# Output projection by seven block products for two token tiles, in place of eight

## The chip, the cores and the metric

The kernel runs on one core of one Trainium2 chip. The metric is the device time of one execution in microseconds (us); three runs of the kernel before took 950.98, 951.33 and 952.13 us, so the time before is the median, 951.33 us.

## What is computed

One decoder layer over 2048 tokens of width 1024, in fp32. A linear recurrence (HGRN2, four heads of 128) gives the first 512 columns of `mix`, sliding-window attention gives the other 512. Then comes the part that the change is about:

```python
mix = jnp.concatenate([o_h, o_a], axis=-1)            # (T, 1024)
out = jnp.einsum('bte,ed->btd', mix, w_out[layer])     # 1024 x 1024
z = DN_ALPHA * h_res.astype(f32) + out.astype(f32)
mu = jnp.mean(z, axis=-1, keepdims=True)
var = jnp.mean(jnp.square(z - mu), axis=-1, keepdims=True)
z = (z - mu) * lax.rsqrt(var + LN_EPS)
h_res = (z * ln_g[layer].astype(f32) + ln_b[layer].astype(f32)).astype(dt)
```

`o_h` is multiplied by a weight per column before; the kernel puts that weight (`hgw_s`) into the first four row blocks of `w_out`.

## The kernel before

The kernel works in three stages: attention (two key/value heads, four token blocks of 512 each), the recurrence (two pairs of heads, index `j`, again four token blocks `b`), and the output stage (16 token tiles of 128). The first two leave their results in DRAM tiles (`sw_spill`, `hg_spill`); the output stage reads them back.

All projections split both fp32 operands into a high part in the fp32r format and a low part, the remainder. A product is three matmuls: high by high, high by low, low by high. ScalarE makes the high part by a copy into fp32r (L97), VectorE or GpSimd subtracts for the low part (L98).

In the output stage `prepare(n)` (L333) loads one token tile `m` with four DMAs from SyncE's queue (L336, L337), has TensorE transpose the four recurrence blocks into PSUM (L342), and splits the eight blocks into `mh` and `ml` (L343 to L346). A token tile then has two halves of 512 output columns; each is a chain of 24 matmuls of 128x128 by 128x512 into one PSUM bank (L537 to L539, eight row blocks `e` by three). VectorE adds the residual (L540, `xr` is loaded by L513), takes statistics (L541, L543), GpSimd makes the reciprocal root (L545, L546), VectorE normalizes with two operations per half (L550, L551), and ScalarE's queue stores (L553, L555). The last token tile is cut into 512, 256 and 256 columns.

The eight row blocks of `w_out` are loaded and split by `load_wo` (L349): six of them, and the first `prepare`, are written into the last step of the recurrence (L421, L422, at `j == 1`, the last block, `pr == 1`), the other two behind it (L509). They go into the buffers of the recurrence's weights (pool `wp`, eight buffers) and tokens (pool `xp`, seven). Every raw tile, of weights, of tokens and of `m`, passes through `rawp`, 4 KB per partition and three buffers.

The order of work on each engine is not the order of the source. A planner simulates a time line when the kernel is built (`schedule_with_timeline_sim=True`): among the instructions that are ready it takes the one that stands first in the source. Buffers of one tag are given out in the order of the source, so the tile n of a tag waits until tile n - bufs is released. Each engine then runs its list in that order.

The projection of the recurrence's values in the last block (`vg`, L120 to L122) reads the weights `wv` in four buffers of `wp`, and `xs` in four of `xp`. After it come, per pair of token tiles, the masked products `ap` (L444, L447), the transposes `kp` (L454), the state update `hkv` (L475), and the outputs `ho` (L488, L492).

Of the kernel before, what the change touches and what calls it, by code (L numbers as in the profile page):

```python
# [10 lines left out]
F32 = mybir.dt.float32  # L11
# [6 lines left out]
P = 128  # L18
# [21 lines left out]
def tile_hybrid_layer(  # L40
# [17 lines left out]
    rawp = ctx.enter_context(tc.tile_pool(name="rawp", bufs=3))  # L58
    wp = ctx.enter_context(tc.tile_pool(name="wp", bufs=8))
# [122 lines left out]
    hk = ctx.enter_context(tc.tile_pool(name="shared", bufs=2))  # L182
# [150 lines left out]
    def prepare(n):  # L333
        m = rawp.tile([P, 8, P], F32, tag="raw", name=f"m{n}")
        for j in range(2):
            nc.sync.dma_start(m[:, 2 * j : 2 * j + 2, :], hg_spill[n // 2][j][n % 2])  # L336
            nc.sync.dma_start(m[:, 4 + 2 * j : 6 + 2 * j, :], sw_spill[n][j])  # L337
        mh = xp.tile([P, 8, P], F32R, tag="xh", name=f"mh{n}")
        ml = xp.tile([P, 8, P], F32R, tag="xl", name=f"ml{n}")
        mp = tr_ps(f"mp{n}")  # L340
        for e in range(4):
            nc.tensor.transpose(mp[:, e, :], m[:, e, :], ident)  # L342
        nc.scalar.activation(mh[:, 0:4, :], mp, AF.Copy)  # L343
        nc.vector.tensor_sub(ml[:, 0:4, :], mp, mh[:, 0:4, :].bitcast(F32))
        nc.scalar.activation(mh[:, 4:8, :], m[:, 4:8, :], AF.Copy)
        nc.vector.tensor_sub(ml[:, 4:8, :], m[:, 4:8, :], mh[:, 4:8, :].bitcast(F32))  # L346
        return mh, ml

    def load_wo(e):  # L349
        pool, tag = (wp, "w") if e < 4 else (xp, "x")  # L350
        return load_split(wo[e], pool, tag, f"wo{e}", scale=hgw_s[:, e : e + 1] if e < 4 else None)

# [1 line left out]
    with (  # L354
# [9 lines left out]
        for j in range(2):  # L364
# [4 lines left out]
            for b in range(NTB):  # L369
# [49 lines left out]
                for pr in range(NBLK // 2):  # L419
                    if j == 1 and b == NTB - 1 and pr == 1:  # L420
                        ws = [load_wo(e) for e in range(6)]  # L421
                        ahead = prepare(0)  # L422
# [86 lines left out]
    ws += [load_wo(e) for e in range(6, 8)]  # L509
    with tc.tile_pool(name="outp", bufs=2, reuse_waits="tile") as wk:  # L510
        def load_res(n):
            xr = wk.tile([P, D], F32, tag="xr", name=f"xr{n}")
            nc.sync.dma_start(xr, xn[n * P : (n + 1) * P, :])  # L513
            return xr

        xrs = [load_res(0), load_res(1)]
        lg = wk.tile([P, D], F32, name="lg", bufs=1)
        nc.sync.dma_start(lg, lng.to_broadcast([P, D]))
        lbt = wk.tile([P, D], F32, name="lbt", bufs=1)
        nc.sync.dma_start(lbt, lnb.to_broadcast([P, D]))  # L520
        for n in range(T // P):
            mh, ml = ahead
            if n + 1 < T // P:
                ahead = prepare(n + 1)
            last = n + 1 == T // P
            xr = xrs.pop(0)
            if n + 2 < T // P:
                xrs.append(load_res(n + 2))
            z = wk.tile([P, D], F32, tag="z", name=f"z{n}")
            cuts = [0, 512, 768, 1024] if last else [0, 512, 1024]  # L530
            stats = wk.tile([P, len(cuts) - 1, 6], F32, tag="bst", name=f"bst{n}")
            for i, (c0, c1_) in enumerate(zip(cuts, cuts[1:])):
                c = slice(c0, c1_)
                ps = mm_ps(f"po{n}_{i}")[:, : c1_ - c0]
                for e in range(8):
                    wh, wl = ws[e]
                    nc.tensor.matmul(ps, lhsT=mh[:, e, :], rhs=wh[:, c], start=e == 0, stop=False)  # L537
                    nc.tensor.matmul(ps, lhsT=mh[:, e, :], rhs=wl[:, c], start=False, stop=False)  # L538
                    nc.tensor.matmul(ps, lhsT=ml[:, e, :], rhs=wh[:, c], start=False, stop=e == 7)  # L539
                nc.vector.scalar_tensor_tensor(z[:, c], xr[:, c], ALPHA, ps, op0=ALU.mult, op1=ALU.add)  # L540
                nc.vector.bn_stats(stats[:, i, :], z[:, c])  # L541
            mv = wk.tile([P, 2], F32, tag="mv", name=f"mv{n}")
            nc.vector.bn_aggr(mv, stats)  # L543
            rs = wk.tile([P, 1], F32, tag="rs", name=f"rs{n}")
            nc.gpsimd.tensor_scalar(rs, mv[:, 1:2], LN_EPS, None, op0=ALU.add)  # L545
            nc.gpsimd.tensor_tensor(rs, rs, mhalf[:, 0:1], op=ALU.pow)  # L546
            y = wk.tile([P, D], F32, tag="y", name=f"y{n}")
            for half in range(2):
                c = slice(half * 512, (half + 1) * 512)
                nc.vector.scalar_tensor_tensor(y[:, c], z[:, c], mv[:, 0:1], lg[:, c], op0=ALU.subtract, op1=ALU.mult)  # L550
                nc.vector.scalar_tensor_tensor(y[:, c], y[:, c], rs, lbt[:, c], op0=ALU.mult, op1=ALU.add)  # L551
                if last:
                    nc.scalar.dma_start(out[n * P : (n + 1) * P, c], y[:, c])  # L553
# [72 lines left out]
```

## Time and profile before

| what | value |
|---|---|
| median of three runs | 951.33 us |
| the profiled execution | span 951.3 us; the runs show no time outside it that could be told apart (median less span: 0.03 us) |
| TensorE busy | 933.0 us, 98% |
| VectorE busy | 607.3 us, 64% |
| ScalarE busy | 308.4 us, 32% |
| GpSimd busy | 322.0 us, 34% |
| the chain that ended last | TensorE 85%, VectorE 6%, DMA 4%, ScalarE 3% |
| matmuls L537, L538, L539 | 264 each (248 with 512 columns and 16 with 256) |

In rows of the profile, PE is TensorE's matmul, PEld its weight load, DVE VectorE, ACT ScalarE, POOL GpSimd, SP SyncE; a q behind a name is that engine's queue. L12 is line 12 of the kernel. Matmuls overlap in the pipeline, so the time from start to start counts, not the length of one.

### The profile page before, as it was taken

What the parts mean: (1) busy time and instruction counts of PE and PEld (TensorE: products, weight loads), DVE (VectorE), ACT (ScalarE), POOL (GpSimd) and SP (SyncE); (2) the same over time, 40 slices, a digit from 0 to 9 for tenths busy, and PEclk for the clock granted to TensorE, in tenths of its full rate; (3) what the DMA queues carried; (4) which work ended last, traced back from release to release, by engine and by line L of the source; (5) the groups of instructions that cost most, each with busy time, mean ns of one, the idle gap of its engine ahead of it and who ended that gap; (6) DMA issues with size and microseconds to landing.
All of it is one profiled execution on the core that took longest, in us unless ns stands there. A gap on an engine that the chain in (4) does not pass through costs nothing.

```text
span 951.3 us, 12917 instructions
## 1 busy us (share of the span) xinstructions
PE 933.0 (98%) x4744; PEld 750.7 (79%) x4744; DVE 607.3 (64%) x1233; ACT 308.4 (32%) x785; POOL 322.0 (34%) x306
## 2 busy tenths in 40 slices
PE   8999999999998999999999999999999989999996
PEld 7878777777786777878887887888788878888885
DVE  5877887867879955726366383726458446666554
ACT  5455545544564423131142423122133211000000
POOL 1645536445447534313042642313133111111111
PEclk9999999999999999999999999999999999999998
DMA  7423243033242403002032321103013253444321
GB/s 261 165 72 123 70 158 124 33 106 106 78 151 94 127 12 101 23 12 100 1 122 78 100 100 65 47 1 102 10 56 123 78 188 134 143 152 146 113 99 57
DMA packets 33216, 91.03 MB, mean 96 GB/s; under 512 B 4224, under 2 KB 12416, under 8 KB 33152
## 3 DMA queue, kind: packets, MB, share of 16 engines
q1 hardware_dynamic: 27792, 73.41, 23.7%
q0 software_dynamic: 2912, 8.40, 2.5%
q10 hardware_dynamic: 2448, 8.39, 2.2%
q8 instruction: 37, 0.61, 0.3%
q14 instruction: 27, 0.22, 0.1%
HBM read 73.41 MB, written 16.78 MB: 95 GB/s over the span
## 4 chain that ended last, share of the span: by engine, by line
PE 85%; DVE 6%; DMA 4%; ACT 3%; issue 1%; SPq 0%; POOL 0%; POOLq 0%; DVEq 0%; ACTq 0%
PE vg L121 6%; PE vg L120 6%; PE vg L122 6%; PE po L537 6%; PE po L539 6%; PE po L538 6%; PE fp L110 3%; PE fp L111 3%; PE fp L112 3%; PE hq L112 3%; PE hq L110 3%; PE hq L111 3%; PE op L320 3%; PE qp L112 2%; PE qp L110 2%; PE qp L111 2%
## 5 line engine op out<-in xcount | busy, mean ns | idle before, releaser
L537 PE MATMUL po<-wo_h,mh 128*128 128x512 f32 (+1 forms) x264 | 103.1, 391 | 2.8 <-DVE z L540 2.8
L539 PE MATMUL po<-wo_h,ml 128*128 128x512 f32 (+1 forms) x264 | 102.0, 386 | 0.0
L538 PE MATMUL po<-wo_l,mh 128*128 128x512 f32 (+1 forms) x264 | 101.9, 386 | 0.0
L120 PE MATMUL vg<-wh_h,xh_h 128*128 128x512 f32 x256 | 100.8, 394 | 0.0
L121 PE MATMUL vg<-wh_l,xh_h 128*128 128x512 f32 x256 | 100.8, 394 | 0.0
L122 PE MATMUL vg<-wh_h,xh_l 128*128 128x512 f32 x256 | 100.7, 394 | 0.0
L98 POOL TENSOR_TENSOR xh_l<-xh_raw,xh_h 128x1024 fp32r<-128x1024 f32 x16 | 39.1, 2448 | 125.6 <-ACT xh_h L97 122.9
L540 DVE SCALAR_TENSOR_TENSOR z<-xr,po 128x512 f32<-128x512 f32 (+1 forms) x33 | 22.1, 672 | 70.3 <-PE po L539 64.3
L545 POOL TENSOR_SCALAR rs<-mv 128x1 f32<-128x1 f32 x16 | 9.4, 584 | 151.4 <-DVE mv L543 151.4
L283 ACT ACTIVATE wt<-sp,st 128x128 f32<-128x128 f32 x128 | 45.8, 365 | 44.4 <-DVE st L279 44.0
L537 PEld LDWEIGHTS po<-wo_h,mh 128*128 128x128 f32 x264 | 50.1, 190 | 12.4 <-DVE z L540 3.0
L293 POOL TENSOR_TENSOR wt<-wt,st 128x512 f32<-128x512 f32 x32 | 37.4, 1169 | 61.9 <-DVE st L292 35.2
L539 PEld LDWEIGHTS po<-wo_h,ml 128*128 128x128 f32 x264 | 50.0, 189 | 10.1
L538 PEld LDWEIGHTS po<-wo_l,mh 128*128 128x128 f32 x264 | 50.0, 189 | 9.5
L343 ACT ACTIVATE mh<-mp 128x512 fp32r<-128x512 f32 x16 | 9.6, 599 | 144.8 <-PE mp L342 144.8
L120 PEld LDWEIGHTS vg<-wh_h,xh_h 128*128 128x128 f32 x256 | 48.4, 189 | 10.1 <-issue 0.6
L121 PEld LDWEIGHTS vg<-wh_l,xh_h 128*128 128x128 f32 x256 | 48.1, 188 | 10.2 <-issue 0.6
L122 PEld LDWEIGHTS vg<-wh_h,xh_l 128*128 128x128 f32 x256 | 48.1, 188 | 9.9 <-issue 0.4
L395 DVE RECIPROCAL re<-e 128x512 f32<-128x512 f32 x16 | 53.5, 3344 | 0.0
L433 DVE SCALAR_TENSOR_TENSOR hg<-tg,vg 128x256 f32<-128x256 f32 x32 | 13.4, 420 | 60.2 <-ACT tg L431 60.2
L110 PE MATMUL fp<-xh_h,wh_h 128*128 128x512 f32 x128 | 51.2, 400 | 0.0
L110 PE MATMUL qp<-xa_h,wa_h 128*128 128x512 f32 x128 | 50.7, 396 | 0.0
(173 smaller groups left out, 2483.9 us busy)
## 6 DMA issues: line engine op xcount, KB each, us to landing
xh_raw<-in_xt_dram SPq DMA_DIRECT2D x32, 512.0 KB, 3.6
xa_raw<-in_xt_dram SPq DMA_DIRECT2D x28, 512.0 KB, 3.7
wh_raw<-in_wt_dram SPq DMA_DIRECT2D x16, 512.0 KB, 3.4
xr<-in_xn_dram SPq DMA_DIRECT2D x16, 512.0 KB, 3.6
out_dram<-y ACTq DMA_DIRECT2D x15, 512.0 KB, 2.6
wa_raw<-in_wt_dram SPq DMA_DIRECT2D x9, 512.0 KB, 4.9
cs<-in_rope_dram SPq DMA_DIRECT2D x8, 512.0 KB, 3.4
sw_spill<-mix POOLq DMA_DIRECT2D x32, 128.0 KB, 2.5
```

The source lines that it names most:

```text
L98: engines[lo_eng].tensor_sub(lo[:, c], raw[:, c], hi[:, c].bitcast(F32))
L110: nc.tensor.matmul(ps, lhsT=wh[:, r], rhs=xh[:, c], start=k == 0, stop=False)
L111: nc.tensor.matmul(ps, lhsT=wh[:, r], rhs=xl[:, c], start=False, stop=False)
L112: nc.tensor.matmul(ps, lhsT=wl[:, r], rhs=xh[:, c], start=False, stop=k == KT - 1)
L120: nc.tensor.matmul(ps, lhsT=xh[:, r], rhs=wh[:, c], start=k == 0, stop=False)
L121: nc.tensor.matmul(ps, lhsT=xh[:, r], rhs=wl[:, c], start=False, stop=False)
L122: nc.tensor.matmul(ps, lhsT=xl[:, r], rhs=wh[:, c], start=False, stop=k == KT - 1)
L283: nc.scalar.activation(wt_[:, s, :], sps[s // 2][:, s % 2, P:], AF.Exp, bias=st[:, 1, s : s + 1], scale=0.125, accum_out=st[:, 3, s : s + 1],)
L395: nc.vector.reciprocal(re, e[:, :, 1:129])
L537: nc.tensor.matmul(ps, lhsT=mh[:, e, :], rhs=wh[:, c], start=e == 0, stop=False)
L538: nc.tensor.matmul(ps, lhsT=mh[:, e, :], rhs=wl[:, c], start=False, stop=False)
L539: nc.tensor.matmul(ps, lhsT=ml[:, e, :], rhs=wh[:, c], start=False, stop=e == 7)
```

## The change

Two token tiles (A) and all of `w_out` (B) are cut into two by two blocks: A into 128 tokens by 512 columns, B into 512 by 512. Seven products of sums of such blocks (called units 1 to 7; Winograd's form) replace eight products of blocks. A unit is four row blocks by three matmuls, 12 matmuls with 512 columns.

- **The weights.** `load_wo` loads a row block in raw form; ScalarE, no longer VectorE, multiplies with `hgw_s`. `wo_first` makes the B sides of units 1, 2 and 6 and stands where the six loads stood; `wo_rest` makes those of units 5, 7, 3 and 4 and stands behind the recurrence. Each loads all eight row blocks, through `rawp`.
- **The tokens.** `prepare(i)` loads both token tiles of pair `i`, transposes as before, copies the transposed half into the raw tile, and makes seven A sides: four sums (two on VectorE, two on GpSimd) and seven splits, in a pool of seven buffers that stands where the recurrence's pools and `hk` stood. No `prepare` stands inside the recurrence any more; the first two follow `wo_rest`.
- **The products.** The residual is loaded as four tiles `z` per pair, and `take` adds a PSUM bank to a `z` tile. Two banks per pair are accumulated on after they were taken: unit 6, 7 and 4 go on in the bank of unit 1, unit 3 in that of unit 5. Each unit is followed by one `take` (seven per pair), four of them with statistics.
- **Layer norm.** ScalarE applies the mean and the reciprocal root, VectorE multiplies by `lg`, GpSimd adds `lbt` and stores; in the last pair VectorE adds and ScalarE's queue stores. The last token tile is no longer cut finer.

```diff
-    hk = ctx.enter_context(tc.tile_pool(name="shared", bufs=2))
+    hk = early_pools.enter_context(tc.tile_pool(name="shared", bufs=2, reuse_waits="tile"))
...
+    def load_wo(e, name):
+        raw = rawp.tile([P, 1024], F32, tag="raw", name=f"wo{e}{name}_raw")
+        nc.sync.dma_start(raw, wo[e])
+        if e < 4:
+            nc.scalar.activation(raw, raw, AF.Copy, scale=hgw_s[:, e : e + 1])
+        return raw[:, 0:512], raw[:, 512:1024]
...
+    def put(unit, e, src, lo_eng="d"):
+        if (unit, e // 2) not in made:
+            pool, tag = (wp, "w") if len(made) in (0, 1, 2, 6, 7, 8, 9, 10) else (xp, "x")
+            made[unit, e // 2] = tuple(
+                pool.tile([P, 2, 512], F32R, tag=f"{tag}{p}", name=f"wo_{unit}_{e // 2}{p}") for p in "hl"
+            )
+        h, l = (t[:, e % 2] for t in made[unit, e // 2])
+        nc.scalar.activation(h, src, AF.Copy)
+        engines[lo_eng].tensor_sub(l, src, h.bitcast(F32))
+
+    def wo_tmp(name):
+        return hk.tile([P, 512], F32, tag="sw", name=f"wot_{name}")
+
+    def wo_first():
         for e in range(4):
...
+            b11, b12 = load_wo(e, "a")
+            b21, b22 = load_wo(e + 4, "a")
+            put(1, e, b11)
+            put(2, e, b21)
+            t2 = wo_tmp(f"f{e}")
+            nc.vector.tensor_sub(t2, b12, b11)
+            nc.vector.tensor_sub(t2, b22, t2)
+            put(6, e, t2)
+
+    def wo_rest():
+        for e in range(4):
+            b11, b12 = load_wo(e, "b")
+            b21, b22 = load_wo(e + 4, "b")
+            t1 = wo_tmp(f"r{e}")
+            nc.vector.tensor_sub(t1, b12, b11)
+            put(5, e, t1)
+            nc.vector.tensor_sub(b12, b22, b12)
+            put(7, e, b12)
+            put(3, e, b22)
+            nc.vector.tensor_sub(t1, b22, t1)
+            nc.vector.tensor_sub(b21, b21, t1)
+            put(4, e, b21)
...
                     if j == 1 and b == NTB - 1 and pr == 1:
-                        ws = [load_wo(e) for e in range(6)]
-                        ahead = prepare(0)
+                        wo_first()
...
-    ws += [load_wo(e) for e in range(6, 8)]
+    wo_rest()
+    early_pools.close()
     with tc.tile_pool(name="outp", bufs=2, reuse_waits="tile") as wk:
...
+        def w_split(src, name):
+            w = wk.tile([P, 2, 512], F32R, tag="m", name=name, bufs=7)
+            nc.scalar.activation(w[:, 0], src, AF.Copy)
+            nc.vector.tensor_sub(w[:, 1], src, w[:, 0].bitcast(F32))
+            return w
+
+        def prepare(i):
+            raws = []
+            for n in (2 * i, 2 * i + 1):
+                m = rawp.tile([P, 8, P], F32, tag="raw", name=f"m{n}")
+                for j in range(2):
+                    nc.sync.dma_start(m[:, 2 * j : 2 * j + 2, :], hg_spill[i][j][n % 2])
+                    nc.sync.dma_start(m[:, 4 + 2 * j : 6 + 2 * j, :], sw_spill[n][j])
+                mp = tr_ps(f"mp{n}")
+                for e in range(4):
+                    nc.tensor.transpose(mp[:, e, :], m[:, e, :], ident)
+                nc.scalar.activation(m[:, 0:4, :], mp, AF.Copy)
+                m = m.rearrange("p e t -> p (e t)")
+                raws.append((m[:, 0:512], m[:, 512:1024]))
+            (a11, a12), (a21, a22) = raws
+            n = f"m{i}"
+            w = {1: w_split(a11, f"{n}_1"), 2: w_split(a12, f"{n}_2")}
+            s1, s2 = (wk.tile([P, 512], F32, tag="tmp", name=f"{n}_s{k}", bufs=2) for k in range(2))
+            nc.vector.tensor_add(s1, a21, a22)
+            nc.vector.tensor_sub(s2, s1, a11)
+            w[6] = w_split(s2, f"{n}_6")
+            w[5] = w_split(s1, f"{n}_5")
+            nc.gpsimd.tensor_sub(s1, a11, a21)
+            w[7] = w_split(s1, f"{n}_7")
+            nc.gpsimd.tensor_sub(s2, a12, s2)
+            w[3] = w_split(s2, f"{n}_3")
+            w[4] = w_split(a22, f"{n}_4")
+            return w
...
+                        t = wk.tile([P, 512], F32, tag="z", name=f"z{i}_{r}{c}", bufs=10)
+                        nc.sync.dma_start(t, xn[(2 * i + r) * P : (2 * i + r + 1) * P, c * 512 : (c + 1) * 512])
...
+            def mul(self, ps, unit, first):
+                for e in range(4):
+                    q = slice(e * P, (e + 1) * P)
+                    ah, al = self.w[unit][:, 0, q], self.w[unit][:, 1, q]
+                    bh, bl = (t[:, e % 2] for t in made[unit, e // 2])
+                    kw = {"skip_group_check": not first}
+                    nc.tensor.matmul(ps, lhsT=ah, rhs=bh, start=first and e == 0, stop=False, **kw)
+                    nc.tensor.matmul(ps, lhsT=ah, rhs=bl, start=False, stop=False, **kw)
+                    nc.tensor.matmul(ps, lhsT=al, rhs=bh, start=False, stop=e == 3, **kw)
+
+            def take(self, r, c, ps, scale=True, done=False):
+                t = self.z[r, c]
+                if scale:
+                    nc.vector.scalar_tensor_tensor(t, t, ALPHA, ps, op0=ALU.mult, op1=ALU.add)
+                else:
+                    nc.vector.tensor_add(t, ps, t)
+                if done:
+                    nc.vector.bn_stats(self.stats[r][:, c, :], t)
+
+            def norm(self, r):
...
+                nc.vector.bn_aggr(mv, self.stats[r])
...
+                nc.gpsimd.tensor_scalar(rs[:, 0:1], mv[:, 1:2], LN_EPS, None, op0=ALU.add)
+                nc.gpsimd.tensor_tensor(rs[:, 0:1], rs[:, 0:1], mhalf[:, 0:1], op=ALU.pow)
+                nc.vector.scalar_tensor_tensor(rs[:, 1:2], mv[:, 0:1], -1.0, rs[:, 0:1], op0=ALU.mult, op1=ALU.mult)
+                for c in range(2):
...
+                    nc.scalar.activation(t, t, AF.Identity, scale=rs[:, 0:1], bias=rs[:, 1:2])
+                    nc.vector.tensor_mul(t, t, lg[:, cs])
+                    (nc.vector if last else nc.gpsimd).tensor_add(t, t, lbt[:, cs])
+                    (nc.scalar if last else nc.gpsimd).dma_start(out[n * P : (n + 1) * P, cs], t)
+
+            def first(self):
+                self.px = mm_ps(f"ox{self.i}")
+                self.mul(self.px, 1, True)
+                self.take(0, 0, self.px)
+
+            def second(self):
+                py = sc_ps(f"oy{self.i}")
+                self.mul(py, 2, True)
+                self.take(0, 0, py, scale=False, done=True)
+
+            def rest(self):
+                px = self.px
+                self.mul(px, 6, False)
+                self.take(0, 1, px)
+                pz = sc_ps(f"oz{self.i}")
+                self.mul(pz, 5, True)
+                self.take(1, 1, pz)
+                self.mul(px, 7, False)
+                self.take(1, 1, px, scale=False, done=True)
+                self.mul(pz, 3, False)
+                self.take(0, 1, pz, scale=False, done=True)
+                self.norm(0)
+                self.mul(px, 4, False)
+                self.take(1, 0, px, done=True)
+                self.norm(1)
+
+        ahead = [Tiles(i, prepare(i)) for i in range(2)]
...
+        for t in ahead:
+            t.first()
+        for t in ahead:
+            t.second()
+        for i in range(T // P // 2):
+            t = ahead.pop(0)
+            if 2 <= i + 1 < T // P // 2:
+                ahead.append(Tiles(i + 1, prepare(i + 1)))
+            if i >= 2:
+                t.first()
+                t.second()
+            t.rest()
```

## Rows read from the trace of the kernel before

**Rows 1.** The page, busy us by engine (share of the span), instructions.
```profile
PE 933.0 (98%) x4744; PEld 750.7 (79%) x4744; DVE 607.3 (64%) x1233; ACT 308.4 (32%) x785; POOL 322.0 (34%) x306
```
**Rows 2.** The chain that ended last, in order of time: start us, us, what.
```profile
770.48 6.03 DMA xr<-in_xn_dram
776.64 0.70 DVE z L540
...
806.97 0.44 PE mp L342 x4
...
818.33 0.44 PE mp L342 x4
```
**Rows 3.** Windows: from:to us, busy us by engine, granted clock, DMA.
```profile
100.00:200.00 100.00, 99.07 (x525) 77.25 (x525) 80.10 (x172) 53.44 (x146) 51.31 (x45) 1.00 0.34 115
...
778.40:781.80 3.40, 3.40 (x9) 2.61 (x8) 3.40 (x8) 0.00 (x0) 0.82 (x2) 0.50 0.97 358
```
**Rows 4.** Timeline of PE, end of the recurrence: start us, us, what.
```profile
751.23 0.39 PE L122 MATMUL vg<-wh_h,xh_l 128*128 128x512 f32 x1
...
753.87 0.48 PE L537 MATMUL po<-wo_h,mh 128*128 128x512 f32 x1
...
758.98 0.61 PE L475 MATMUL hkv<-hv,kt 128*128 128x128 f32 x4
...
763.94 0.39 PE L492 MATMUL ho<-u,kq 128*128 128x128 f32 x2
```
**Rows 5.** Timeline of DVE beside it.
```profile
754.13 0.73 DVE L456 COPY_PREDICATED at<-tri,ap 64x512 f32<-64x512 int32 x1
754.87 0.45 DVE L457 COPY_PREDICATED at<-tri,ap 64x256 f32<-64x256 int32 x1
```
**Rows 6.** Timeline of SP's queue: start us, us, DMA issues.
```profile
726.73 0.42 SPq L337 DMA_DIRECT2D m<-sw_spill  x1
729.48 2.00 SPq L94 DMA_DIRECT2D wo_raw<-in_wo_dram  x2
```
**Rows 7.** DMA issues by tile, KB each, median us from issue to landing.
```profile
wo_raw<-in_wo_dram SPq DMA_DIRECT2D x8, 512.0 KB, 3.6
...
m<-sw_spill SPq DMA_DIRECT2D x32, 128.0 KB, 3.3
```
**Rows 8.** Waits of SP's queue: us in total, times, longest us.
```profile
SPq L94 <- DVE wo_l L98: 27.6, 5, 13.2
```
**Rows 9.** Timeline of DVE, back to back in the output stage.
```profile
779.04 0.67 DVE L344 TENSOR_TENSOR ml<-mp,mh 128x512 fp32r<-128x512 f32 x1
779.63 0.68 DVE L540 SCALAR_TENSOR_TENSOR z<-xr,po 128x512 f32<-128x512 f32 x1
780.22 0.20 DVE L543 BATCH_NORM_AGGREGATE mv<-bst 128x2 f32<-128x12 f32 x1
780.34 0.69 DVE L541 BATCH_NORM_STATS2 bst<-z 128x6 f32<-128x512 f32 x1
```
**Rows 10.** Groups by form, ACT, 800 to 940 us: busy us, mean ns.
```profile
L343 ACT ACTIVATE mh<-mp 128x512 fp32r<-128x512 f32 x11 | 6.6, 599 | 112.7 <-PE mp L342 112.7
```
**Rows 11.** Timeline of POOL and DVE, subtractions of both at once.
```profile
110.91 4.74 POOL L98 TENSOR_TENSOR xa_l<-xa_raw,xa_h 128x1024 fp32r<-128x1024 f32 x2
...
111.66 5.07 DVE L98 TENSOR_TENSOR xa_l<-xa_raw,xa_h 128x1024 fp32r<-128x1024 f32 x1 [1.59 <-ACT xa_h L97]
```
**Rows 12.** Groups by form, DVE, 20 to 320 us: busy us, mean ns, idle before.
```profile
L98 DVE TENSOR_TENSOR xa_l<-xa_raw,xa_h 128x1024 fp32r<-128x1024 f32 x14 | 25.9, 1849 | 10.7 <-ACT xa_h L97 10.7
...
L212 DVE TENSOR_TENSOR rot_q<-rot_q,sw_q 128x512 f32<-128x512 f32 x16 | 10.7, 670 | 1.2 <-POOL sw_q L210 1.2
...
L98 DVE TENSOR_TENSOR wa_l<-wa_raw,wa_h 128x1024 fp32r<-128x1024 f32 x7 | 8.7, 1240 | 7.9 <-ACT wa_h L97 7.9
```
**Rows 13.** Timeline, the end of the span.
```profile
943.22 0.42 DVE L540 SCALAR_TENSOR_TENSOR z<-xr,po 128x256 f32<-128x256 f32 x1 [1.99 <-PE po L539]
...
946.29 1.42 DVE L551 SCALAR_TENSOR_TENSOR y<-y,rs,lbt 128x512 f32<-128x512 f32 x2 [0.46 <-POOL rs L546]
```

More of the change, by code (lines that the diff above doesn't have):

```diff
@@ L58, in tile_hybrid_layer @@
     rawp = ctx.enter_context(tc.tile_pool(name="rawp", bufs=3))
+    early_pools = ctx.enter_context(ExitStack())
     wp = ctx.enter_context(tc.tile_pool(name="wp", bufs=8))
@@ L330, in tile_hybrid_layer @@
                 prev_k, prev_v = (kh, kl), v
[L333 to L340, printed above, removed]
-        for e in range(4):
[L342 to L347, printed above, removed]
@@ L349, in load_wo @@
-    def load_wo(e):
-        pool, tag = (wp, "w") if e < 4 else (xp, "x")
-        return load_split(wo[e], pool, tag, f"wo{e}", scale=hgw_s[:, e : e + 1] if e < 4 else None)
+    def load_wo(e, name):
[4 more added lines that the diff above has]
+        return raw[:, 0:512], raw[:, 512:1024]
+    made = {}
+    def put(unit, e, src, lo_eng="d"):
[7 more added lines that the diff above has]
+        engines[lo_eng].tensor_sub(l, src, h.bitcast(F32))
@@ L506, in tile_hybrid_layer, with __init__ @@
                     nc.gpsimd.dma_start(hg_spill[b * 2 + pr][j].rearrange("i p h d -> p i h d"), mix)
-    ws += [load_wo(e) for e in range(6, 8)]
+    wo_rest()
+    early_pools.close()
     with tc.tile_pool(name="outp", bufs=2, reuse_waits="tile") as wk:
[L511 to L516, printed above, removed]
-        lg = wk.tile([P, D], F32, name="lg", bufs=1)
+        lg = wk.tile([P, D], F32, name="lg", bufs=1)
+        lbt = wk.tile([P, D], F32, name="lbt", bufs=1)
+        def w_split(src, name):
[30 more added lines that the diff above has]
+            return w
+        class Tiles:
+            def __init__(self, i, w):
+                self.i, self.w = i, w
+                self.z = {}
+                for r in range(2):
+                    for c in range(2):
+                        t = wk.tile([P, 512], F32, tag="z", name=f"z{i}_{r}{c}", bufs=10)
+                        nc.sync.dma_start(t, xn[(2 * i + r) * P : (2 * i + r + 1) * P, c * 512 : (c + 1) * 512])
+                        self.z[r, c] = t
+                self.stats = [wk.tile([P, 2, 6], F32, tag="bst", name=f"bst{i}_{r}", bufs=4) for r in range(2)]
+            def mul(self, ps, unit, first):
[16 more added lines that the diff above has]
+            def norm(self, r):
+                n = 2 * self.i + r
+                last = self.i == T // P // 2 - 1
+                mv = wk.tile([P, 2], F32, tag="mv", name=f"mv{n}")
+                nc.vector.bn_aggr(mv, self.stats[r])
+                rs = wk.tile([P, 2], F32, tag="rs", name=f"rs{n}")
+                nc.gpsimd.tensor_scalar(rs[:, 0:1], mv[:, 1:2], LN_EPS, None, op0=ALU.add)
+                nc.gpsimd.tensor_tensor(rs[:, 0:1], rs[:, 0:1], mhalf[:, 0:1], op=ALU.pow)
+                nc.vector.scalar_tensor_tensor(rs[:, 1:2], mv[:, 0:1], -1.0, rs[:, 0:1], op0=ALU.mult, op1=ALU.mult)
+                for c in range(2):
+                    t = self.z[r, c]
+                    cs = slice(c * 512, (c + 1) * 512)
+                    nc.scalar.activation(t, t, AF.Identity, scale=rs[:, 0:1], bias=rs[:, 1:2])
[26 more added lines that the diff above has]
+        ahead = [Tiles(i, prepare(i)) for i in range(2)]
@@ L518, in tile_hybrid_layer @@
         nc.sync.dma_start(lg, lng.to_broadcast([P, D]))
-        lbt = wk.tile([P, D], F32, name="lbt", bufs=1)
         nc.sync.dma_start(lbt, lnb.to_broadcast([P, D]))
[L521 to L553, printed above, removed]
-            if not last:
-                nc.scalar.dma_start(out[n * P : (n + 1) * P, :], y)
```

## The prediction

> **What bounds the kernel now.** I read the page first: PE is busy 98% of the span, no other engine over two thirds [rows 1], so the end is set by what PE has to do and where it stands still. The chain of waits in order of time says where that is in the output stage: two pieces `mp` (the transposes of one token tile) stand 11.36 us apart, from 806.97 to 818.33, and so it goes on in a regular step to the end; earlier it leaves PE only at 770.48, for the load of `xr` and the first residual addition [rows 2]. So a token tile costs PE 11.36 us: 0.44 of transposes and 10.92 for 48 matmuls, 0.2275 us each. (One matmul row is 0.39 us long, but they overlap.) The stretch behind that stall ran at a granted clock of 0.50, the lower of the two levels (1.2 GHz), and held 9 matmul starts in 3.4 us, where 15 would fit [rows 3]. The timeline of PE at the seam tells how it is hidden: the last `vg` matmul starts at 751.23, the first `po` at 753.87, and the recurrence's last `hkv` and `ho` (758.98, 763.94) lie among `po` matmuls, for which the first token tile and six weight blocks were ready [rows 4].
>
> **The steady part.** Before, a pair of token tiles takes 2 x 11.36 = 22.72 us. After, it has 84 matmuls in place of 96, with the same shape: 84 x 0.2275 + 2 x 0.44 = 19.99, say 20.0 us. Over eight pairs the gain is 21.8 us. That is the whole gain of the change.
>
> Can the others keep up with 20.0 us per pair? DVE starts one 512-wide instruction every 0.59 to 0.61 us, reading PSUM or SBUF [rows 9]. A pair has 7 low parts, 2 sums, 7 takes, 4 statistics, 4 products with `lg`: 24 x 0.60 = 14.4, and four small ones at about 0.15: 15.0 us. ACT has 2 copies, 7 splits, 4 normalizations at 0.6 [rows 10], 8 us, and is no bound. GpSimd is new in this stage: 2 differences and 4 additions; 1024-wide ones took 4.74 for two [rows 11], so 1.19 for 512, 7.1 us per pair.
>
> These meet DVE. While the two subtractions ran on GpSimd, a subtraction on DVE took 5.07 us [rows 11]; where GpSimd did not subtract beside it the mean is 1.24 (`wa_l`), for `xa_l` 1.85, and `rot_q`, also two operands in SBUF, had 0.67 [rows 12]. DVE has 13 such instructions in a pair (low parts, sums, products), 7.8 us. Below: none of it lengthened, 15.0. Above: DVE stands still for all of GpSimd's 7.1, 22.1, more than PE's 20.0. Between plus 49% (`xa_l` against `wa_l`) and plus nothing (`rot_q`) I take plus 30%, 2.3 us: 17.3 of 20.0, 87%. With DVE at 80 of 100 us and GpSimd at 51, PE was still busy for 99 [rows 3]. For 87% I take waits of 0.3 us per pair, 2.4 in all; the ends are 0 and 8 x 2.1 = 17.
>
> A page speaks against the change here. The Trainium skill (SBUF — State Buffer, section "Who interferes with whom") says that a VectorE instruction with two SBUF inputs contends with a GpSimd instruction that reads SBUF, and that the later one waits until the other has finished. The 5.07 us of [rows 11] agree. By that rule alone the sum would be nearer the upper end, which is rival A.
>
> **The seam.** Here the change gives back. Before, `prepare(0)` stood ahead of the last weights, and so in the queue (its last load at 726.73, weights 6 and 7 at 729.48) [rows 6]: buffers of `rawp` are given in the source's order. After, the order in these three buffers is eight halves of `wo_first`, eight of `wo_rest`, then `m0`, `m1`. Already six blocks made SP wait 27.6 us for low parts, in five waits [rows 8]. PE has nothing of the output stage to do until `m0` is in, transposed and split.
>
> When is that? `wo_first` needs `hk`'s buffers after the recurrence's last gates, but by my count of its loads the second half for `wo_rest`'s first block lands near 746. That block's units 7, 3 and 4 need the buffers of `wv`, which the last 24 `vg` matmuls (746.1 to 751.5, by 0.2275 from [rows 4]) free one by one; unit 7 is written near 749, and only then is its raw buffer free. From there each block costs a load (0.2 to issue, 3.6 to land [rows 7]) and the way from landing to the release of the buffer, difference, high and low part: 3 x 0.6 and three handoffs of 0.2, 2.4. So the second halves of blocks 1, 2, 3 land at 752.8, 759.8, 767, two of them with 0.8 to 0.9 for the recurrence's DVE work between (1.18 at 754.13 alone [rows 5]). `m0` takes the buffer of block 2's second half, released 5.9 after it landed (eight DVE instructions and that work), at 765.7. Its recurrence part is there 3.5 later (four issues of 0.4, landing 2 to 3.3 [rows 6, 7]), at 769.2. Transposes 0.44, ACT's copy and split at 0.6 each [rows 10], handoffs: PE starts unit 1 at **771.5**. Ends: 766 with no handoffs and nothing of the recurrence between, 779 if `wo_first` is 7 us late or the loads queue up.
>
> PE's recurrence ends earlier without `po` between: transposes to 754, DVE's two masks to 755.3 [rows 5], `hkv`, state, `ho`, about 757.8. So PE stands still for about 14 us, which `po` matmuls filled before [rows 4]. What else is late next: units 1 and 2 need only `m0`; unit 6 needs `m1`, released about 3 us behind `m0`, its sums and split, near 778; units 1 and 2 last until 778.6. I add nothing. After the gap PE begins on the lower level; I take what it cost after the short stall, 9 starts where 15 fit [rows 3], 3.4 / 2 = 1.7 us, ends 0 and 3.4.
>
> **The end.** From the last residual addition's start to the end of the span it is 951.3 - 943.22 = 8.1 us [rows 13]. After, addition and statistics are on 512, not 256 columns: 2 x 0.27 more. A small product on DVE comes in (0.2 with its handoff), ACT's normalization (0.7), and four DVE instructions of 0.6 in place of two in 1.42 [rows 13], 1.0 more: 2.4, with a handoff 2.5. So 10.6; ends 9 and 12.
>
> **The sum**, on the profiled execution's time line: 771.5 + 8 x 20.0 - 0.5 (the first transposes lie ahead of it) + 1.7 + 2.4 + 10.6 = 945.7, against its span of 951.3. That span is the median of the runs to 0.03 us, so nothing is added: **946 us**. Code ahead of the seam has the same PE work, fewer wide DVE scalings and more ACT work; ACT is at a third of the span, and I cost that at nothing (the planner's new order may move it by 1 us either way).
>
> **Rivals.**
> A, the other side: DVE stands still for GpSimd. Place: each pair, where `lbt` additions and differences meet low parts and products. It decides from 5.0 us of DVE standstill per pair (15.0 + 5.0 = 20.0), and the kernel is slower than before from 6.2. Price at the upper end: 8 x 22.1 = 176.8 in place of 160.0 + 2.4: 945.7 + 14.4 = **960**. For it: 5.07 us. Against: `rot_q` at 0.67, the planner, and that many DVE instructions in between read PSUM. Chance 0.15.
> B: the seam is longer, PE starts near 779: **953**. For it: SP's waits, three buffers. Against: the loads of one block do overlap with the split of the one before. Chance 0.15, half of it within 0.2% of before or faster.
> C: the seam is shorter than I think, unit 1 starts by 764 since the planner has all weights made earlier: **938**. For it: only unit 1's and 2's weights are needed, and those are early. Against: `rawp`'s order. Chance 0.10.
> D: a unit that goes on in a bank must wait for its take. Between stands one other unit, 2.73 us, for a take of 0.7 and what stands ahead of it on DVE; with two or three instructions ahead it is late. At 1 us per pair: 946 + 8 - 2.4 = **951**. Against: the next pair's units 1 and 2 have banks of their own and may go in between. Chance 0.10.
>
> **How the numbers follow.** The forecast, 941 to 949.4, has 0.50. What a measurement can tell from no change is 0.2%, 1.9 us: faster is under 949.4, slower over 953.2. Faster: 0.50 + 0.10 (C) + 0.03 (B) + 0.03 (D) = 0.66. Same: 0.02 (A) + 0.07 (B) + 0.05 (D) = 0.14. Slower: 0.13 + 0.05 + 0.02 = 0.20. The range 938 to 957 leaves out most of A and half of C. The forecast's own range is 941 to 949.
>
> **What would show it.** 672 matmuls of the units, 84 of them and eight transposes in 20 us; DVE over 85% busy behind the seam, some of its two-operand rows near 1.2 us or more beside GpSimd; PE idle for 10 to 18 us from about 758, ended by a token split whose load waited for a buffer; the clock's lower level behind it; 10 to 11 us from the last matmul to the end. It is wrong if pairs take over 21 us (A or D; PE's waits then name DVE's takes), or if unit 1 starts among the recurrence's last `ho` (C).

## The result, and the profile after

The changed kernel takes 958.02 us (median of four runs, 957.04 to 961.91), the kernel before in the same session 951.15 us (949.12 to 952.13). The ratio is 1.0083, 95% interval 1.0060 to 1.0105: slower by 0.8%, where 946 us and faster was forecast, and 1 us above the range.

The profiled execution has a span of 955.3 us and took 957.04. The page of the changed kernel, busy us by engine, against [rows 1]:

```profile
PE 917.8 (96%) x4624; PEld 731.8 (77%) x4624; DVE 669.9 (70%) x1323; ACT 370.2 (39%) x885; POOL 390.5 (41%) x378
```

TensorE has 120 instructions less and is busy 15 us less, and the span is longer: the work went, the time did not. Three stretches say where it stayed.

**The seam.** Changed kernel, PE's timeline behind the recurrence, against [rows 4]:

```profile
759.96 0.39 PE L519 MATMUL ho<-u,kq 128*128 128x128 f32 x2
769.17 0.66 PE L558 MATMUL mp<-ident,m 128*128 128x128 f32 x2 [8.82 <-DMA m<-hg_spill]
...
772.82 0.79 PE L594 MATMUL ox<-wo_0h,m 128*128 128x512 f32 x1
```

and SP's queue ahead of it:

```profile
748.69 0.33 SPq L336 DMA_DIRECT2D wo5b_raw<-in_wo_dram  x1
749.98 0.33 SPq L336 DMA_DIRECT2D wo2b_raw<-in_wo_dram  x1
757.53 0.33 SPq L336 DMA_DIRECT2D wo6b_raw<-in_wo_dram  x1
759.13 0.33 SPq L336 DMA_DIRECT2D wo3b_raw<-in_wo_dram  x1
763.93 0.33 SPq L336 DMA_DIRECT2D wo7b_raw<-in_wo_dram  x1
766.76 0.33 SPq L554 DMA_DIRECT2D m<-hg_spill  x1
```

The first unit starts at 772.82, 12.5 us behind the recurrence's last output. The loads of the weights' second halves (`wo5b`, `wo6b`, `wo7b`) are 8.8 and 6.4 us apart, and `m0` comes behind all of them: the chain through three raw buffers, as forecast.

**The pairs.** Windows of the changed kernel (from:to us, busy us of each engine with its instructions, granted clock, DMA share, GB/s) show what [rows 3] showed for attention:

```profile
840.00:860.00 20.00, 19.41 (x88) 15.43 (x88) 18.49 (x27) 7.50 (x13) 12.16 (x15) 1.00 0.47 155
880.00:900.00 20.00, 18.76 (x87) 14.88 (x86) 17.91 (x28) 6.83 (x12) 11.57 (x14) 1.00 0.49 158
900.00:920.00 20.00, 19.94 (x89) 15.87 (x88) 19.25 (x28) 6.36 (x11) 13.41 (x15) 1.00 0.40 126
```

VectorE is busy 18 to 19 of 20 us and GpSimd 12 to 13. A busy VectorE row counts the time in which the instruction stands still. The groups of VectorE from 790 to 930 us (line, tiles, shapes, count, busy us, mean ns, idle before) say which instructions got longer:

```profile
L620 DVE TENSOR_TENSOR z<-z,lg 128x512 f32<-128x512 f32 x24 | 28.0, 1180 | 5.2 <-ACT z L619 5.2
L545 DVE TENSOR_TENSOR m<-m_s,m 128x512 fp32r<-128x512 f32 x28 | 26.1, 954 | 1.5 <-ACT m L544 1.2
L605 DVE BATCH_NORM_STATS2 bst<-z 128x6 f32<-128x512 f32 x27 | 18.3, 679 | 0.0
...
L601 DVE SCALAR_TENSOR_TENSOR z<-z,ox 128x512 f32<-128x512 f32 x19 | 12.7, 671 | 0.1
L566 DVE TENSOR_TENSOR m_s<-m 128x512 f32<-128x512 f32 x7 | 7.4, 1061 | 3.3 <-ACT m L559 3.3
```

The statistics (one operand) and the takes (one operand in PSUM) have 0.67 to 0.68 us as in [rows 9]; products, low parts and sums, with both operands in SBUF, have means of 954 to 1180 ns. Single instructions show why. VectorE's timeline:

```profile
910.16 0.69 DVE L620 TENSOR_TENSOR z<-z,lg 128x512 f32<-128x512 f32 x1 [0.24 <-ACT z L619]
910.77 0.69 DVE L605 BATCH_NORM_STATS2 bst<-z 128x6 f32<-128x512 f32 x1
911.37 1.40 DVE L620 TENSOR_TENSOR z<-z,lg 128x512 f32<-128x512 f32 x1
912.70 0.68 DVE L545 TENSOR_TENSOR m<-m,m 128x512 fp32r<-128x512 f32 x1
913.30 1.77 DVE L566 TENSOR_TENSOR m_s<-m 128x512 f32<-128x512 f32 x1
```

and GpSimd's beside it:

```profile
910.93 1.29 POOL L621 TENSOR_TENSOR z<-z,lbt 128x512 f32<-128x512 f32 x1 [1.85 <-DVE z L620]
912.85 1.68 POOL L621 TENSOR_TENSOR z<-z,lbt 128x512 f32<-128x512 f32 x1 [0.63 <-DVE z L620]
```

The product at 910.16 ran alone, 0.69 us; the statistics at 910.77 ran beside an addition, 0.69 too; the product at 911.37 met the addition that had begun at 910.93, ended 0.55 us after it and took 1.40; the sum at 913.30 met the next one, ended 0.54 us after it and took 1.77. So it is in the whole stretch: from 790 to 930 us, 34 wide VectorE instructions with both operands in SBUF began while a wide GpSimd instruction ran, and 33 of them ended 0.55 us after its end, whatever was left of it, with 0.81 to 1.79 us each (the other began 0.03 us before that end). The 13 that a GpSimd instruction joined later, and the 38 that met none, have 0.63 to 0.69. They are not slowed, they wait until GpSimd is done. GpSimd's own groups there:

```profile
L621 POOL TENSOR_TENSOR z<-z,lbt 128x512 f32<-128x512 f32 x24 | 36.4, 1526 | 15.5 <-DVE z L620 15.5
L572 POOL TENSOR_TENSOR m_s<-m,m_s 128x512 f32<-128x512 f32 x7 | 11.3, 1620 | 20.4 <-DVE m L545 18.2 <-DMA z<-in_xn_dram 2.2
```

The product is what the addition waits for, so the first addition of a token tile starts just ahead of the tile's second product.

What that did to TensorE, its waits from 790 to 946 us (what, released by: us in total, times, longest):

```profile
PE ox L594 <- DVE mv L611: 2.3, 1, 2.3
PE mp L558 <- DMA m<-hg_spill: 1.2, 2, 0.9
PE ox L594 <- DVE z L603: 0.8, 2, 0.4
PE ox L594 <- DVE z L601: 0.5, 1, 0.5
```

The longest is in the last pair:

```profile
933.64 0.66 DVE L601 SCALAR_TENSOR_TENSOR z<-z,ox 128x512 f32<-128x512 f32 x1
934.45 0.64 PE L594 MATMUL ox<-wo_0h,m 128*128 128x512 f32 x1 [2.33 <-DVE mv L611]
```

By the order of the source this matmul opens unit 7, which goes on in the bank of unit 6, so it waits for the take at 933.64; `mv` is the small VectorE instruction that ended just before it. A stretch on the lower clock follows (granted clock 0.50 from 934.6 to 938.0), in which 12 matmuls took 4.4 us against 2.7. The waits listed are 4.8 us and the lower clock 1.7; what else the pairs lost (below) stands in no row of waits.

**The end.** The last take begins at 944.51, 10.8 us before the end of the span (8.1 in [rows 13]).

### The profile page after: what moved, and what is told of

Read it like the earlier page. It is cut to its first block, busy times and chain, and to the rows that moved or that the text cites. A ratio compares the mean times of both kernels' runs of the same rounds, so it can differ in the third digit from the quotient of the medians.

```text
span 955.3 us, 13062 instructions
## 1 busy us (share of the span) xinstructions
PE 917.8 (96%) x4624; PEld 731.8 (77%) x4624; DVE 669.9 (70%) x1323; ACT 370.2 (39%) x885; POOL 390.5 (41%) x378
## 4 chain that ended last, share of the span: by engine, by line
PE 69%; DVE 16%; DMA 5%; issue 4%; ACT 3%; POOL 2%; SPq 1%; DVEq 0%; ACTq 0%; POOLq 0%
PE vg L121 6%; PE vg L122 6%; PE vg L123 6%; PE fp L111 3%; PE fp L112 3%; PE hq L113 3%; PE fp L113 3%; PE hq L111 3%; PE hq L112 3%; DVE m L545 3%; PE op L321 2%; PE qp L113 2%; PE qp L111 2%; PE qp L112 2%; PE gp L111 2%
## 5 line engine op out<-in xcount | busy, mean ns | idle before, releaser
L456 ACT ACTIVATE hv<-vg 128x256 f32<-128x256 f32 x32 | 12.2, 380 | 102.2 <-PE vg L123 102.2
L112 PE MATMUL gp<-xa_l,wa_h 128*128 128x512 f32 x128 | 50.8, 397 | 0.0
L113 PE MATMUL gp<-xa_h,wa_l 128*128 128x512 f32 x128 | 50.8, 397 | 0.0
L111 PE MATMUL hq<-xh_h,wh_h 128*128 128x512 f32 x128 | 50.7, 396 | 0.0
L113 PE MATMUL qp<-xa_h,wa_l 128*128 128x512 f32 x128 | 50.6, 395 | 0.0
L111 PE MATMUL gp<-xa_h,wa_h 128*128 128x512 f32 x128 | 50.5, 394 | 0.0
L113 PE MATMUL hq<-xh_h,wh_l 128*128 128x512 f32 x128 | 50.4, 394 | 0.0
L112 PE MATMUL qp<-xa_l,wa_h 128*128 128x512 f32 x128 | 50.4, 394 | 0.0
L112 PE MATMUL hq<-xh_l,wh_h 128*128 128x512 f32 x128 | 50.3, 393 | 0.0
```

The lines of the kernel that those rows point to most:

```text
L111: nc.tensor.matmul(ps, lhsT=wh[:, r], rhs=xh[:, c], start=k == 0, stop=False)
L112: nc.tensor.matmul(ps, lhsT=wh[:, r], rhs=xl[:, c], start=False, stop=False)
L113: nc.tensor.matmul(ps, lhsT=wl[:, r], rhs=xh[:, c], start=False, stop=k == KT - 1)
```

## The experiments

All were timed beside the kernel before. In the short diffs, + and - are against the changed kernel where nothing else is said. The first question was whether GpSimd's wide instructions cost the time (rival A), the second what holds the seam.

**All wide GpSimd work on VectorE.**

```diff
-            nc.gpsimd.tensor_sub(s1, a11, a21)
+            nc.vector.tensor_sub(s1, a11, a21)
...
-            nc.gpsimd.tensor_sub(s2, a12, s2)
+            nc.vector.tensor_sub(s2, a12, s2)
...
-                    (nc.vector if last else nc.gpsimd).tensor_add(t, t, lbt[:, cs])
+                    nc.vector.tensor_add(t, t, lbt[:, cs])
```

> GpSimd's two differences per pair and its additions of lbt go to VectorE; GpSimd keeps the small root operations and the stores. Theory L (VectorE stands still while GpSimd reads SBUF): VectorE gets 6 more instructions of 0.6 us per pair (15.0 + 3.6 = 18.6 us of PE's 20.0) but no standstill, so the groups of low parts and of products with lg fall from means of 0.95 and 1.18 to 0.65 to 0.70 us, and the time falls by 2 to 6 us against the changed kernel. Rival N (the count of VectorE instructions decides): 18.6 is more work than before, waits grow, the time rises by 2 to 5 us.

Measured: 949.64 us, ratio to before 0.9984 (0.9974 to 0.9993), 8.4 us under the changed kernel, more than the 2 to 6 put down for theory L. Its windows and, from 790 to 930 us, groups of VectorE:

```profile
880.00:900.00 20.00, 20.00 (x94) 16.45 (x93) 18.72 (x35) 8.12 (x13) 4.39 (x8) 1.00 0.47 154
900.00:920.00 20.00, 20.00 (x92) 16.55 (x91) 18.98 (x36) 7.80 (x12) 4.39 (x8) 1.00 0.33 116
```

```profile
L605 DVE BATCH_NORM_STATS2 bst<-z 128x6 f32<-128x512 f32 x28 | 18.9, 686 | 0.0
L545 DVE TENSOR_TENSOR m<-m_s,m 128x512 fp32r<-128x512 f32 x28 | 18.4, 686 | 0.1
L620 DVE TENSOR_TENSOR z<-z,lg 128x512 f32<-128x512 f32 x26 | 17.6, 682 | 0.0
L621 DVE TENSOR_TENSOR z<-z,lbt 128x512 f32<-128x512 f32 x26 | 17.5, 686 | 0.0
```

VectorE does about 35 instructions in 20 us in place of 28, every group of wide ones has a mean of 0.68 to 0.69 us, TensorE does not stand still in these windows, and the trace names no wait of TensorE from 790 us to the end. So VectorE's larger count of instructions was no hindrance; GpSimd's wide instructions were.

**The additions of `lbt` left out, or alone moved.** The first run leaves the additions out in all pairs but the last:

```diff
-                    (nc.vector if last else nc.gpsimd).tensor_add(t, t, lbt[:, cs])
+                    if last:
+                        nc.vector.tensor_add(t, t, lbt[:, cs])
```

> The addition of lbt is left out in all pairs but the last, so GpSimd has 2 wide operations per pair in place of 6 and VectorE nothing more. It prices GpSimd's additions alone. Theory L: VectorE's busy share behind the seam falls from 97% to about 83%, PE's waits in the pairs and the 2.3 us wait of the last pair go, time 5 to 8 us under the changed kernel. Rival N: VectorE's work is unchanged, so 0 to 1 us.

Measured: 949.46 us (0.9982, 0.9972 to 0.9993), 8.6 us under the changed kernel; VectorE's busy share from 790 to 930 us falls from 89 to 83% (not from 97). The second moves the additions to VectorE and leaves the differences on GpSimd:

```diff
-                    (nc.vector if last else nc.gpsimd).tensor_add(t, t, lbt[:, cs])
+                    nc.vector.tensor_add(t, t, lbt[:, cs])
```

> From the changed kernel only GpSimd's additions of lbt go to VectorE; the two differences per pair stay on GpSimd. If the additions carry nearly all of the loss (leaving them out gave as much as taking all wide work away), 949 to 951. If the differences cost as much each (1.3 us of standstill, twice per pair), 952 to 955.

Measured: 952.9 us (1.0018, 1.0007 to 1.0029), in the second of the two ranges put down. Taking the additions off GpSimd gives 5.1 of the 8.4 us, the differences as well the other 3.3. In the first of the two runs the products still have a mean of 1080 ns beside the differences (group of VectorE, 790 to 930 us):

```profile
L620 DVE TENSOR_TENSOR z<-z,lg 128x512 f32<-128x512 f32 x26 | 27.8, 1080 | 3.5 <-ACT z L619 3.5
```

but VectorE has four instructions less per pair, and TensorE has no wait. In the second, with them, TensorE has one:

```profile
PE ox L594 <- DVE z L601: 2.4, 1, 2.4
```

It lies in the last pair (929.23), and the lower clock follows it again (0.50 from 929.5 to 932.9): 2.4 and 1.7 us, nearly all of the 4.6 by which this run's way from first unit to last take is longer than that of the run without wide GpSimd work. The rows fit a simple reading, that VectorE's standstill costs nothing while it has room (busy 83% of 790 to 930 us in the first run) and something when it has little (93% in the second); no run varies the room alone.

**The seam: `m0` and `m1` in the seventh buffer of `xp`**, in place of `rawp`.

```diff
-                m = rawp.tile([P, 8, P], F32, tag="raw", name=f"m{n}")
+                if i == 0:
+                    m = xp.tile([P, 8, P], F32, tag="xh" if n == 0 else "xl", name=f"m{n}")
+                else:
+                    m = rawp.tile([P, 8, P], F32, tag="raw", name=f"m{n}")
```

> Only the raw buffers of the first pair change: m0 and m1 go into the seventh buffer of the token pool, free near 751, instead of waiting in rawp behind the eight halves of wo_rest. Theory S (the 13 us gap is that wait): the first unit starts near 757 to 762 instead of 772.8, unit 5 waits for its weights till about 768, the gap shrinks to 3 to 6 us, time 7 to 12 us under the changed kernel. Rival M (the A sides wait for memory that the recurrence and the weights' temporaries hold till the end, or VectorE does wo_rest first): unit 1 still starts after 769 and the time stays within 2 us.

Measured: 957.15 us (1.0058, 1.0042 to 1.0074); the interval overlaps the changed kernel's. SP's queue of this run shows the first reason:

```profile
759.01 0.33 SPq L336 DMA_DIRECT2D wo6b_raw<-in_wo_dram  x1
760.61 0.33 SPq L336 DMA_DIRECT2D wo3b_raw<-in_wo_dram  x1
761.03 0.38 SPq L557 DMA_DIRECT2D m<-hg_spill  x1
761.46 0.42 SPq L558 DMA_DIRECT2D m<-sw_spill  x1
765.56 0.33 SPq L336 DMA_DIRECT2D wo7b_raw<-in_wo_dram  x1
765.99 0.38 SPq L557 DMA_DIRECT2D m<-hg_spill  x1
```

`m0` has a buffer of its own and still stands in the queue behind weights that wait for theirs; part of it stands behind `wo7b` and lands at 769.3. A second reason follows on ScalarE: `m0` is transposed and copied by 771.0, but its split comes behind the copy of `m1`, which waits for its transposes, and a split of weights:

```profile
773.60 1.14 ACT L544 ACTIVATE m<-m 128x512 fp32r<-128x512 f32 x2
```

The first unit began at 774.27. The same edit with the first experiment's:

> Both of the above together. If S and L are separate places, the gains add up: 9 to 18 us under the changed kernel, so 940 to 949, under the kernel before. If N holds it is slower than the seam alone.

Measured: 948.31 us (0.9973, 0.9961 to 0.9986).

**The first pair ahead of `wo_rest`**, on top of that; `wo_rest`'s temporaries go into the output stage's pool:

```diff
-    wo_rest()
     early_pools.close()
...
-        ahead = [Tiles(i, prepare(i)) for i in range(2)]
+        ahead = [Tiles(0, prepare(0))]
+        wo_rest(lambda name: wk.tile([P, 512], F32, tag="tmpw", name=name, bufs=2))
+        ahead.append(Tiles(1, prepare(1)))
```

> No wide GpSimd work, m0 and m1 in the token pool's seventh buffer, and the first pair's preparation written ahead of the second half of the weights, so that its loads stand ahead of those loads in SyncE's queue. In the run with the seam's buffers alone the first two loads were issued at 761.0, behind the loads for wo_rest (759.0, 760.6), though the buffer was free near 752. Theory S' (the queue and the order, not the memory, hold back the first pair): first unit starts at 756 to 762, units 1, 2 and 6 of the first pair fill 8 us of the gap, the rest of that pair follows the weights near 772 to 776; 5 to 9 us under the 949.6 us of the run without GpSimd. Rival M (the A sides wait for memory that the recurrence holds): first unit after 768, within 2 us of 949.6.

Measured: 959.53 us (1.0086, 1.0070 to 1.0103), where 5 to 9 us under 949.6 was expected. The first unit did begin at 761.27, but the temporaries now lie in the output stage's memory, which the recurrence holds to its end: the last `hmix` ran to 763.28 and the first temporary was written at 763.79. `wo_rest` slid with them; `wo5b` was issued at 773.96, behind the loads of `z`, in place of 750.19. TensorE's waits from 755 to 800 us:

```profile
PE ox L596 <- ACT wo_0h L350: 4.6, 1, 4.6
PE ox L596 <- ACT wo_1h L350: 3.5, 1, 3.5
PE ox L598 <- DVE m L544: 3.1, 1, 3.1
PE mp L560 <- DMA m<-hg_spill: 2.9, 1, 2.9
```

The same with the norm as before, two VectorE operations and no ScalarE step:

```diff
-                    nc.scalar.activation(t, t, AF.Identity, scale=rs[:, 0:1], bias=rs[:, 1:2])
-                    nc.vector.tensor_mul(t, t, lg[:, cs])
+                    nc.vector.scalar_tensor_tensor(t, t, mv[:, 0:1], lg[:, cs], op0=ALU.subtract, op1=ALU.mult)
...
-                    nc.vector.tensor_add(t, t, lbt[:, cs])
+                    nc.vector.scalar_tensor_tensor(t, t, rs, lbt[:, cs], op0=ALU.mult, op1=ALU.add)
```

> As the run with the first pair early, and the layer norm as in the kernel before: two VectorE operations per half, no ScalarE step, no small product. VectorE's wide instructions stay at 30 per pair. The end of the span, 10.8 us from the last matmul in the changed kernel, should shrink by the ScalarE step and its handoffs, to 9 to 9.5, so 1 to 2 us less than that run.

Measured: 960.04 us (1.0089, 1.0073 to 1.0105): no difference from the run before it that these intervals could show. The expectation failed in its mechanism too: from the last take to the end it is 12.1 us, against 10.8 in the run before it and not 9 to 9.5. The statistics behind the last take (946.61) begin only at 948.53, since VectorE does two norm operations of the other token tile (947.20, 1.41 us) ahead of them.

**Only units 1 and 2 of the first pair early, `wo_rest` in its place.** Against the combined kernel of 948.31 us (`head` is the part of `prepare` up to the splits of units 1 and 2, `mul` as in the diff above):

```diff
-    wo_rest()
+    wo_rest(range(2))
+    head0 = head(0, lambda u: hk.tile([P, 2, 512], F32R, tag=f"q{u - 1}", name=f"m0_{u}"))
+    px0, py0 = mm_ps("ox0"), sc_ps("oy0")
+    mul(px0, head0[1], 1, True)
+    mul(py0, head0[1], 2, True)
+    wo_rest(range(2, 4))
```

> Edit: e3b_seam_no_pool (all wide GpSimd work on VectorE, m0 and m1 in xp's seventh buffer) with the first two units of pair 0 taken out of the seam's queues without moving wo_rest: the splits of units 1 and 2 of pair 0 stand in the spare buffers of the recurrence's tags q0 and q1 instead of the memory that the recurrence gives up at its end, m0 and m1 are loaded between the second and the third step of wo_rest (behind wo5b, ahead of wo6b), and wo_rest keeps its place and its temporaries. Theory S'' (the empty stretch of TensorE from 762 to 774.5 is one of memory and of a place in SP's queue, not of work that is missing): m0 arrives soon after its buffer is free at about 752, the first unit starts at 757 to 762 instead of 774.5, wo_rest still ends at 772 to 775, and of the 13 us TensorE gets 24 matmuls (5.3 us at 0.222) done and with them some of the cold clock: 948.3 - 5 = 943 (941 to 945). Rival R (the gap only moves, as in e5: after the two units TensorE waits for m2 and m3, which come behind wo7b, and for units 5, 7, 3, 4 of w_out): the first unit is early, the unit after them no earlier than 774, and pair 0's later units wait for weights: 946 to 949. Rival Q (m0 put ahead of wo6b delays the chain of w_out's raw buffers as in e5): wo_rest ends at 780 or later, time 950 or more.

Measured: 948.44 us against 952.25 of the kernel before on that chip (0.9962, 0.9949 to 0.9975). The two intervals to before, this one's and the combined kernel's, overlap. PE's timeline:

```profile
758.74 0.78 PE L398 MATMUL oy<-wo_0h,m 128*128 128x512 f32 x1
...
766.75 0.38 PE L554 MATMUL ho<-u,kq 128*128 128x128 f32 x2
771.25 0.66 PE L384 MATMUL mp<-ident,m 128*128 128x128 f32 x2 [4.12 <-DMA m<-hg_spill]
```

VectorE's, and SP's queue, for what came next:

```profile
779.40 0.69 DVE L622 SCALAR_TENSOR_TENSOR z<-z,ox 128x512 f32<-128x512 f32 x1 [2.66 <-DMA z<-in_xn_dram]
```

```profile
766.01 0.33 SPq L336 DMA_DIRECT2D wo7b_raw<-in_wo_dram  x1
769.02 0.33 SPq L380 DMA_DIRECT2D m<-hg_spill  x1
...
776.35 3.87 SPq L612 DMA_DIRECT2D z<-in_xn_dram  x8
```

Units 1 and 2 lie among the recurrence's last outputs (758.74 to 766.75), as `po` did before [rows 4]. Then TensorE stands still again, for the second pair's `m`, which comes behind `wo7b`, and up to 780.23 for the take that frees a bank, whose `z` was loaded behind all of these. The gap moved: rival R of the expectation, at its price.

| kernel | first unit | last take | span | time |
|---|---|---|---|---|
| changed | 772.82 | 944.51 | 955.3 | 958.02 |
| no wide GpSimd work | 774.37 | 936.70 | 947.8 | 949.64 |
| additions left out | 775.02 | 937.69 | 948.8 | 949.46 |
| additions alone moved | 772.40 | 939.31 | 949.9 | 952.9 |
| `m` in `xp` | 774.27 | 945.71 | 956.7 | 957.15 |
| `m` in `xp`, no wide GpSimd work | 774.51 | 936.03 | 947.2 | 948.31 |
| first pair ahead of `wo_rest` | 761.27 | 948.50 | 959.3 | 959.53 |
| the same, norm as before | 760.48 | 946.61 | 958.7 | 960.04 |
| units 1 and 2 early | 758.74 | 935.66 | 946.8 | 948.44 |

(First unit, last take and span are us of each profiled execution, time is the median.)

## Why the prediction was wrong

**The step that failed is "for 87% I take waits of 0.3 us per pair, 2.4 in all".** From first unit to last take the sum had 8 x 20.0 - 0.5 + 1.7 + 2.4 = 163.6 us; measured were 171.7, and without wide GpSimd work 162.3. GpSimd's share is 171.7 - 162.3 = 9.4 us in the profiled executions (8.4 in the medians), four times the 2.4. A pair took 21.5 us, over the 21 that was named as the sign of rival A or D: it is rival A's mechanism, at a little over half of the 8 x 2.1 = 16.8 us that it had as its upper end.

Its parts. GpSimd's 7.1 us per pair were too few: it takes 1.29 us for a 512-wide instruction that meets nothing, and additions and differences have means of 1526 to 1620 ns in the changed kernel where 1.19 us was worked out from [rows 11], and with the stores it issues GpSimd is busy 12 to 13 of 20 us. VectorE's standstill I put at 2.3 us per pair; over the seven pairs from 790 to 930 us the means over 0.68 add up to (1180 - 682) x 24 + (954 - 686) x 28 + (1061 - 677) x 7 = 22.1 us, 3.2 per pair (677 is that line's mean with the additions left out). With the 19 low parts `m<-m,m` at 733 and the 13 small products at 326 ns, 154 without GpSimd beside them, it is about 3.6 per pair. That is 1.3 more, and under the 5.0 from which rival A was to decide. What failed is thus the threshold more than the load: I let VectorE be filled to 20.0 us before TensorE waits, on the strength of a window with 80 of 100 us [rows 3]. From 790 to 930 us the kernel without wide GpSimd work has VectorE busy for 126.5 us and TensorE never waits; the changed one has 125.2 and it does. So the busy share could not have told it. What differs is the shape: rows of 1.4 to 1.8 us in an engine that works in order, and a chain through it, ScalarE and GpSimd, on which VectorE itself then waits (5.2 us for L619). That the shape is what makes the takes late is argued from these rows; no run changes it alone.

Between the two ends of the price the rows had 5.07 us on one side and `rot_q` at 0.67 on the other [rows 11, 12]; I went by the middle. `rot_q` was no evidence against: in the trace of before 15 of its 16 rows begin while no GpSimd arithmetic runs. And a percentage on VectorE's rows was the wrong form, since what an instruction loses is what is left of GpSimd's. The Trainium skill (SBUF — State Buffer, section "Who interferes with whom") spoke for rival A, and this case's trace agrees: with two operands in SBUF 0.69 us alone and up to 1.79 when GpSimd came first, with one operand in SBUF 0.67 to 0.69 either way.

Left open: how much of the 9.4 us came through VectorE's longer instructions and how much through GpSimd being late with its own differences and small norm steps. With the additions away the differences were as long as before (1621 ns) and cost TensorE nothing, which speaks for the first.

**Right.** 84 matmuls and eight transposes in 20.0 us: with GpSimd out of the way, 162.3 us from first unit to last take against 161.2 worked out without waits. The seam: 772.82 against 771.5, by the chain of raw buffers that the sum went through; second halves issued at 757.53 and 763.93 and landing at 761.3 and 767.1, where 759.8 and 767 stood. Its small terms are luckier than that: 0.2 for an issue and 0.2 for a handoff stood on no row, and the runs show 0.33 for an issue of weights and 0.03 to 0.08 from the end of one engine's instruction to the start of the next engine's (909.09 to 909.12, 910.85 to 910.93). The end: 10.8 against 10.6. Rivals B and C did not happen; of D's waits for takes there are 3.6 us in the changed kernel (the two rows released by `z`, and the 2.3 us at 934.45), and none without wide GpSimd work. In the rows they are the main way by which A's loss reaches TensorE.

**Small terms.** The lower clock behind the gap (granted 0.50 to 777.6): the first 24 matmuls, of units 1 and 2, took 8.0 us with two transposes between, 2.5 more than 24 x 0.2275, where 1.7 stood (and 9 starts where 15 fit are 1.4 us, not 1.7). And the base: the profiled run of the changed kernel takes 1.7 us more than its span (957.04 against 955.3), and so do later runs of the kernel before (950.6 against 948.9), so the span of 951.3 belonged to an execution of about 953, not to the median; the sum's 945.7 was a span, and as a time it is 947.4.

**Where the gain went.** 21.8 us were there to win, and the kernel without wide GpSimd work shows them won: no wait in the pairs. The seam takes 12.6 us of it (774.37 less 761.74, the start of the last `ho` there), the lower clock 2.5 and the longer end 3.0 (11.1 against 8.1), which leaves 3.7. The spans differ by 951.3 - 947.8 = 3.5. So near a match is in part luck: the account leaves out the stall of the kernel before (2.8 us, and the lower clock behind it), which is gone, and TensorE's waits in the end of the recurrence (3.0 us in that run), which are new. In the medians, where the profiled execution of before was about 2 us over its own, the difference is 1.1, ratio 0.9984. In the changed kernel GpSimd takes 8.4 more and turns the sign.

## What to carry to other kernels

Work that is handed to GpSimd is not taken off VectorE if GpSimd reads SBUF while VectorE has two operands there: count what VectorE may stand still for it, or keep it on VectorE, which here did the same six instructions in 0.69 us each without TensorE waiting. When a change empties the stretch that hid a stage's start, price that stretch as carefully as the gain: the edits that brought the first unit forward, by 13 to 16 us against the kernel they were made in, made the time longer or left it where the intervals can't tell it apart, since buffers, queue order and memory of the stage before stood one behind the other. A busy share below 100% is no proof of room; look for what stands ahead of the one instruction that the bounding engine waits for, here a take.

## What the runs showed that was not expected

- A statistics instruction on an SBUF tile ran 0.69 us beside a GpSimd addition, while the product behind it waited for that same addition (911.37, 1.40 us). A product of one column waits too: with both operands in SBUF it took 1.25 us at 918.34 and ended 0.02 us after a difference on GpSimd.
- A buffer that is free is not enough for a load: `m0`'s stood behind two loads of weights in SP's queue until 761.03, with the next two parts behind a third until 765.99.
- Moving 24 matmuls (5.5 us) into the empty stretch changed the end by less than the intervals can tell.
